# A third set of split weights, a shorter GELU and gate, and new duration formulas in the list scheduler of a two-layer decoder kernel

## The chip, the core and the metric

The kernel runs on one core of a Trainium2 chip. The metric is the device time of one execution in microseconds (us); the median of several runs is given. The engines are named PE (TensorE, the matmuls), PEld (its weight loads), DVE (VectorE), ACT (ScalarE), POOL (GpSimd) and SP (SyncE, whose queue issues the DMAs).

## The reference, cut to what matters

One inference step of a decoder with two layers, 2048 wide, for 592 tokens: 16 meta and 512 prompt tokens (528) and 8 samples of 8 tokens (64). Everything is fp32.

```python
# layer 0: one input projection; a convolution branch and an S5 branch
u_a, g_a, z_a, u_b, z_b = split(x @ ev_w_in)              # 5 x 1024 columns
h   = u_a * sigmoid(g_a)                                  # the gate ("glu")
c   = swish(layernorm(depthwise_conv31(h) + conv_b))      # over 1024 channels
y_a = c @ a_pw
y   = Re(C s5_scan(u_b)) + D * u_b                        # 64 groups of 16, 64 states each
y   = gelu(y)
v, gt = split(y @ glu_w + glu_b);  y_b = v * sigmoid(gt)
mix = concat(y_a * silu(z_a), y_b * silu(z_b))
x   = layernorm(alpha * x + mix @ ev_w_out)
# layer 1: one input projection; mLSTM (4 heads of 256) and RWKV-7 (16 heads of 64)
...
x   = layernorm(alpha * x + mix @ od_w_out)
```

GELU is the tanh form: 0.5 y (1 + tanh(sqrt(2/pi) (y + 0.044715 y^3))). Outputs are the rows of x and the new states of every branch.

## The kernel before

**Dense products.** Features lie on partitions and tokens on columns. Each fp32 product is made of three products of a shorter type (fp32r): the high part of the weights by the high and by the low part of x, and the low part of the weights by the high part of x (in the rows: `acc<-xh,wh`, `acc<-xl,wh`, `acc<-xh,wl`). A weight tile `wraw` (128 x 4 x 128, 256 KB) is loaded by DMA; ACT copies it to `wh`, and DVE subtracts `wh` from it to make `wl`. Each pair feeds 24 matmuls, on 2 column spans of 296 (288 in the RWKV stage). There are two sets of `wh` and `wl`, and a third `wraw` can be loaded ahead. `dense_threads` makes five threads of this: `loads`, `splits`, `products`, `results`, and the jobs that they work through in a fixed order. A job's `then` handles its finished sums in `acc`.

**Order of the work.** Nothing reorders on the chip: each engine runs its queue in program order. The program order within the three manual stages (layer 0; RWKV; mLSTM) comes from a list scheduler, `Weave`. Threads with priorities (a lower number goes first) offer operations; `Weave` keeps a model of every engine's time, takes for each operation the time at which it could start by the model, and emits the one that can start first, priorities deciding among those near each other. The model's durations are in `cost`, and the time from the end of an operation on one engine to the start of its reader on another is in `delay`. So these formulas never change what is computed or how long anything takes; they decide who stands ahead of whom in each queue. Between the stages stand the two output projections, written in a plain order.

**Layer 0.** Jobs: S5 inputs, gates and convolution inputs, gate columns `z`. The S5 branch goes in 8 blocks: tables are made on POOL, PE multiplies (`sps<-s5ul,s5m`, `sps<-s5xpad,s5ca`, `sps<-s5xpad,s5cb`), ACT copies the output to `s5y`, and the GELU of `s5_out` runs over ACT and DVE in tiles `s5q` and `s5y`. `yb` takes the result to DRAM. The convolution's 31 taps are STT (scalar_tensor_tensor) operations on DVE (`taps<-hh,par,taps`). The thread `norms` makes the LayerNorm sums, then waits until all 8 GELU blocks are issued (`len(YB) == 8`), closes the pool that the convolution and S5 used, and makes the operand `C[0]` to `C[7]` of the product `a_pw` one after another: on DVE an STT, on ACT a tanh (`sa`), on DVE a tensor_scalar and an STT (all on `cc`), on ACT the copy `cbh`, on DVE the subtraction `cbl`. The operand Y of the product `glu_w` is loaded back from DRAM and split the same way (`cbh`, `cbl` with strided columns). The first job of `a_pw` needs `C[0]` to `C[7]` in turn (`acc<-cbh`).

**RWKV.** 16 pairs of groups and heads go through: PE products of the group's chunk (`sps<-rar,rbdk` and others); results go through DRAM (`rcd`) and come back as `rcf`; POOL inverts small triangular matrices by a chain of 30 small operations (`rnt<-rcf,rn` and `rn<-rn,rnt`, 15 each); then POOL makes `rlv`, which PE reads. Behind the chain in POOL's queue also stand the low parts `rlo` of the head norms, which PE reads in `sps<-rlo,rcc` and `sps<-rlo,rcb`. A serial chain carries the state over the chunks: `qy<-rgm,rtok`, DVE copies `rqt`, PE transposes (`cp<-cst,rqt`), ACT `rq`, PE `cp<-rtok` and `cp<-rq,rhh`, DVE `rs`, the next `qy`. Dense products of `w_m` and `w_r` fill PE between these. The mLSTM stage follows with the products of `w_g`.

Of the kernel before, what the change touches and what calls it, by code (L numbers as in the profile page):

```python
# [11 lines left out]
F32 = mybir.dt.float32  # L12
# [209 lines left out]
def delay(p, e):  # L222

    if p == e:
        return {"G": 0.1, "D": 2.0}.get(e, 0.0)
    if e == "T":
        return {"A": 0.3, "V": 0.23, "G": 0.2}.get(p, 1.2) + MT
    return {"T": 0.2, "G": 0.08, "D": 1.2}.get(p, 0.14) + (MV if e == "V" else MA)
# [10 lines left out]
def cost(e, fn, out, ins):  # L239

    n = math.prod(out.shape[1:])
    if e == "T":
        if fn == "transpose":
            return 0.12
        return max(n, 256) / 2400 + 0.003 if ins[0].dtype == F32R else max(n / 600 + 0.006, 0.218)
    n = max([n] + [math.prod(z.shape[1:]) for z in ins])
    cols = sum(z.shape[1:] == (1,) for z in ins) * (n > 1)
    if e == "A":
        return 0.05 + n / 1100 + 0.09 * cols
    if e == "G":  # L250
        if fn == "memset":
            return 0.03 + n / 1190
        return 0.13 + n / 300 if fn == "tensor_copy" else max(0.157 + n / 560, 0.055 + n / 417)
    if fn == "reciprocal":
        return 0.07 + n / 160
    fast = fn == "tensor_scalar" and all(z.space != PSUM for z in ins)
    return 0.07 + n / (1920 if fast else 960) + 0.06 * cols

# [333 lines left out]
def s5_setup(K, pool, S):  # L592
# [12 lines left out]
    yield G.memset(S.xpad, 0.0)  # L605
    dt, mag, th = t_("dt"), t_("mag"), t_("th")
    tmp = t_("ean"), t_("ear"), t_("eae", sh, I32)
    yield V.tensor_copy(dt, P["ldt"])
# [3 lines left out]
    yield tt(th, P["lami"], dt, OP.mult)  # L612
    n = t_("n")
    yield V.tensor_scalar(n, th, 1.0 / (2 * math.pi), 12582912.0, op0=OP.mult, op1=OP.add)
# [6 lines left out]
    yield V.tensor_scalar(th, th, 3.1415925, -3.1415925, op0=OP.min, op1=OP.max)  # L621
    sn, cs = t_("sn"), t_("cs")
    yield A.activation(cs, th, AF.Abs)
# [9 lines left out]
    yield V.memset(S.pi[:, :, 0], 0.0)  # L633
    t1, t2 = t_("t1"), t_("t2")
    for k in range(2, 9):
# [167 lines left out]
def s5_out(K, pool, S, j, tables, u, yb, ahead):  # L803
# [30 lines left out]
    q = pool.tile([128, 592], F32, name="s5q", tag="s5u", bufs=4)  # L834
    yield A.square(q, y)
    yield V.tensor_scalar(q, q, 0.044715, 1.0, op0=OP.mult, op1=OP.add)
    yield V.tensor_tensor(q, q, y, op=OP.mult)
    yield A.activation(q, q, AF.Tanh, scale=math.sqrt(2.0 / math.pi))
    yield V.tensor_scalar(y, y, 0.5, None, op0=OP.mult)
    yield V.scalar_tensor_tensor(y, q, 1.0, y, op0=OP.add, op1=OP.mult)  # L840
# [36 lines left out]
def layer0(K, O):  # L877
# [3 lines left out]
    with mk("l0") as p0:  # L881
# [3 lines left out]
        with banks(K, sps=2), mk("ln0") as pl, mk("cc", 8) as pc, mk("zs") as pz, ExitStack() as mid, \  # L885
# [38 lines left out]
            def inputs(j, tag):  # L924
# [10 lines left out]
                return Job(I["w_e"], 24 + j, SPAN0, then, tag=tag, after=after)  # L935

            def glu_gate(j):
                def then(acc):
                    g = cv.tile([128, NT], F32, name="sg")
                    for p, (a, b) in zip(acc, SPAN0):  # L940
                        yield A.activation(g[:, a:b], p, AF.Tanh, scale=0.5)
                    w.give("acc", "acc")
                    yield V.tensor_scalar(g, g, 0.5, 0.5, op0=OP.mult, op1=OP.add)
                    SG.append(g)
                return Job(I["w_e"], 8 + j, SPAN0, then)

            def glu(j):
                b8 = lambda z: z.rearrange("p (b t) -> p b t", b=8)

                def then(acc):  # L950
                    g = SG.popleft()
                    h = cv.tile([128, 862], F32, name="hh", bufs=2)
                    hs = b8(h[:, 558:])
                    yield D.dma_start(hs[:, :, 0:30], I["sconv"][j])
                    yield G.memset(h[:, 0:30], 0.0)
                    yield V.tensor_tensor(h[:, 30:326], g[:, 0:296], acc[0], op=OP.mult)
                    yield V.tensor_tensor(h[:, 326:558], g[:, 296:NP], acc[1][:, 0:232], op=OP.mult)
                    yield V.tensor_tensor(hs[:, :, 30:38], b8(g[:, NP:NT]), b8(acc[1][:, 232:296]), op=OP.mult)
# [5 lines left out]
                return Job(I["w_e"], j, SPAN0, then)  # L964

# [23 lines left out]
            def out(j):  # L989
                def then(acc):  # L990
# [85 lines left out]
            def norms():  # L1076
# [170 lines left out]
class Job:  # L1247
# [3 lines left out]

    def __init__(self, W, s, spans, then, paired=False, final=False, X=None, tag="acc", after=None):
        self.W, self.s, self.spans, self.then, self.paired, self.final = W, s, spans, then, paired, final
        self.after = after
        self.X, self.tag, self.nk = X, tag, W.shape[2] if W is not None else 0


def dense_threads(K, w, jobs, X):


    q = Ctx()
    q.raw, q.w, q.acc, q.nraw, q.nw = deque(), deque(), deque(), 0, 0
    q.loaded, q.freed, q.early = 0, 0, []

# [16 lines left out]
    def splits():  # L1281
        while True:
            yield lambda: q.raw and (q.nw < 2 or q.raw[0] is None)
            item = q.raw.popleft()
# [4 lines left out]
            q.nw += 1  # L1289
            wh, wl = (K.wp.tile([128, 4, 128], F32R, name=m, bufs=2) for m in ("wh", "wl"))  # L1290
            if job.paired:
                yield w.A.copy(wh[:, :, 0:64], raw[:, :, 0:64])
                yield w.V.tensor_tensor(wh[:, :, 64:], raw[:, :, 0:64], wh[:, :, 0:64].bitcast(F32), op=OP.subtract)
            else:
                yield w.A.copy(wh, raw)
                yield w.V.tensor_tensor(wl, raw, wh.bitcast(F32), op=OP.subtract)
            q.nraw -= 1
            q.w.append((wh, wl, job, i0))

    def products():  # L1300
        while True:
            yield lambda: q.w
            item = q.w.popleft()
            if item is None:
                q.acc.append(None)
                return
            wh, wl, job, i0 = item
            if not job.spans:
# [7 lines left out]
            for kk in range(4):  # L1316
# [1051 lines left out]
```

## Time and profile before

| | before |
|---|---|
| median of 3 runs | 2701.41 us (2700.88 to 2701.69) |
| the profiled execution | 2697.97 us; span 2696.0 us |
| mean granted clock of TensorE | 0.986 |
| PE busy | 2586.8 us (96%), 18864 instructions |
| DVE busy | 1637.6 us (61%) |
| ACT busy | 1070.7 us (40%) |
| POOL busy | 1005.3 us (37%) |

The span runs from the first to the last instruction of the profiled execution; its own time is 2 us more. PE is busy nearly all of the time, so the time is the matmuls' work, at the clock that is granted, and PE's idle stretches. Layer 0 runs to about 1030 us (the output projection from about 800), RWKV from there to 1970, mLSTM to about 2480, and the last output projection to the end.

### The profile page before, as it was taken

To read this page: it belongs to the slowest core of one execution; us is meant where nothing else is said; L and a number is where in the kernel's file an instruction comes from. 1 tells how busy PE (TensorE), PEld (TensorE's weight loads), DVE (VectorE), ACT (ScalarE), POOL (GpSimd) and SP (SyncE) were. 2 spreads that over 40 slices of the span, in tenths; PEclk is the share of its full clock that TensorE was granted. 3 is DMA by queue.
4 is the path that set the end of the run, shared out by engine and by line. 5 is a ranking of instruction groups with operands and counts; after the bars stand their busy time and mean duration, and the time that the engine had idled before them with its cause. 6 is when DMAs were issued, how large, how long until landed. Compare 5 with 4: busy or idle time off the path is not lost. (4 is left out here: it accounts for less than half of the span.)

```text
span 2696.0 us, 49549 instructions
## 1 busy us (share of the span) xinstructions
PE 2586.8 (96%) x18864; PEld 2523.7 (94%) x18864; DVE 1637.6 (61%) x3070; ACT 1070.7 (40%) x2313; POOL 1005.3 (37%) x1810
## 2 busy tenths in 40 slices
PE   8998999999999999998999999999999999999997
PEld 8998999899999999998989999999999989898997
DVE  7578986755443356675776757667563544457436
ACT  4322332344232244554554545455333434344223
POOL 1887788720002233343344143244200212212443
PEclk9999999999999999999999999999999999999999
DMA  6433443345333333222222222222333433425333
GB/s 199 104 104 90 110 112 90 103 134 148 110 106 104 107 111 130 80 71 72 71 71 71 75 80 65 69 73 76 97 105 88 140 99 122 145 89 174 109 109 118
DMA packets 202094, 278.31 MB, mean 103 GB/s; under 512 B 66809, under 2 KB 86009, under 8 KB 201857
## 3 DMA queue, kind: packets, MB, share of 16 engines
q1 hardware_dynamic: 199552, 270.30, 33.5%
q10 hardware_dynamic: 2304, 4.85, 0.5%
q8 instruction: 148, 2.42, 0.4%
q14 instruction: 90, 0.73, 0.1%
HBM read 232.54 MB, written 42.53 MB: 102 GB/s over the span
## 5 line engine op out<-in xcount | busy, mean ns | idle before, releaser
L321 PE MATMUL acc<-xh,wh 128*128 128x296 f32 (+1 forms) x3520 | 805.8, 306 | 10.2 <-ACT xh L321 6.5
L321 PE MATMUL acc<-xh,wl 128*128 128x296 f32 (+2 forms) x3488 | 796.4, 305 | 15.2 <-DVE wl L321 15.1
L321 PE MATMUL acc<-xl,wh 128*128 128x296 f32 (+1 forms) x3520 | 802.8, 305 | 0.0
L321 DVE TENSOR_TENSOR wl<-wraw,wh 128x512 fp32r<-128x512 f32 x492 | 385.6, 784 | 373.4 <-ACT wh L321 356.2
L321 PEld LDWEIGHTS acc<-xh,wh 128*128 128x128 f32 x3520 | 584.5, 192 | 15.4 <-ACT xh L321 6.5
L321 PEld LDWEIGHTS acc<-xh,wl 128*128 128x128 f32 x3488 | 577.0, 191 | 19.8 <-DVE wl L321 17.6
L321 PEld LDWEIGHTS acc<-xl,wh 128*128 128x128 f32 x3520 | 583.3, 191 | 1.4 <-issue 0.7
L321 ACT CAST wh<-wraw 128x512 fp32r<-128x512 f32 (+1 forms) x496 | 306.1, 618 | 660.9 <-PE acc L321 592.5
L490 PE MATMUL acc<-xh,wh 128*128 128x296 f32 (+2 forms) x832 | 182.7, 299 | 0.0
L490 PE MATMUL acc<-xl,wh 128*128 128x296 f32 (+2 forms) x832 | 181.9, 297 | 0.7 <-DVE xl L321 0.7
L490 PE MATMUL acc<-xh,wl 128*128 128x296 f32 (+1 forms) x832 | 181.4, 298 | 0.5 <-DVE wl L434 0.5
L321 DVE SCALAR_TENSOR_TENSOR taps<-hh,par,taps 128x528 f32<-128x528 f32 x232 | 178.3, 768 | 4.7
L433 ACT CAST wh<-wraw 128x512 fp32r<-128x512 f32 x100 | 61.9, 621 | 207.8 <-PE acc L490 205.1
L490 PEld LDWEIGHTS acc<-xl,wh 128*128 128x128 f32 x832 | 132.4, 188 | 1.3 <-DVE xl L321 0.9
L490 PEld LDWEIGHTS acc<-xh,wh 128*128 128x128 f32 x832 | 132.4, 189 | 0.5 <-ACT wh L433 0.2
L490 PEld LDWEIGHTS acc<-xh,wl 128*128 128x128 f32 x832 | 131.9, 188 | 0.9 <-DVE wl L434 0.7
L434 DVE TENSOR_TENSOR wl<-wraw,wh 128x512 fp32r<-128x512 f32 x100 | 73.8, 738 | 94.2 <-ACT wh L433 88.6
L321 POOL TENSOR_TENSOR rnt<-rcf,rn 128x75 f32<-128x75 f32 (+14 forms) x240 | 86.5, 360 | 88.7 <-DMA rcf<-rcd 72.3
L404 POOL TENSOR_TENSOR lnb<-lnb,rr 128x592 f32<-128x592 f32 (+1 forms) x24 | 42.4, 1766 | 184.2 <-DVE rr L1155 184.2
L1186 POOL TENSOR_TENSOR rr<-rr,lna 128x592 f32<-128x592 f32 (+1 forms) x2 | 3.5, 1742 | 280.0 <-DMA wraw<-w_eo 254.8
L321 POOL TENSOR_TENSOR k<-mc,mch 128x512 fp32r<-128x512 f32 x32 | 42.9, 1341 | 152.3 <-ACT mch L321 139.8
L321 ACT ACT_TABLE_LOAD x69 | 88.5, 1283 | 18.8 <-DVE rh L321 17.0
(586 smaller groups left out, 4851.9 us busy)
## 6 DMA issues: line engine op xcount, KB each, us to landing
wraw<-w_e SPq DMA_DIRECT2D x160, 256.0 KB, 3.2
wraw<-w_m SPq DMA_DIRECT2D x160, 256.0 KB, 3.1
wraw<-w_r SPq DMA_DIRECT2D x132, 256.0 KB, 3.1
wraw<-w_eo SPq DMA_DIRECT2D x64, 256.0 KB, 3.0
wraw<-w_oo SPq DMA_DIRECT2D x64, 256.0 KB, 3.1
rcf<-rcd SPq DMA_DIRECT2D x16, 640.0 KB
wraw<-w_glu SPq DMA_DIRECT2D x32, 256.0 KB, 2.6
mc<-mc SPq DMA_DIRECT2D x32, 256.0 KB, 3.3
```

The costliest lines, as they stand in the source:

```text
L321: getattr(eng.e, fn)(out, *a, **kw)
L404: getattr(eng.e, fn)(out, *a, **kw)
L433: K.nc.scalar.copy(H, x)
L434: (e or K.nc.vector).tensor_tensor(L, x, H.bitcast(F32), op=OP.subtract)
L490: K.nc.tensor.matmul(o, w[:, kk], x[:, a:b], start=st, stop=sp)
L1186: G.tensor_tensor(r, r, N.c, op=OP.subtract)
```

## The change

Three edits are joined.

1. The formulas in `cost` and `delay` for ACT, POOL and DVE get other numbers. POOL to PE becomes 0.5 instead of 0.2. Small operations become dearer: a DVE operation costs at least 0.2, a POOL operation on two tensors at least 0.25 + n/560, ACT 0.1 + n/1150; an operation of DVE with two tensors in SBUF costs 0.06 more. All three stages are ordered by them.
2. In layer 0 alone there is a third set of split weights (`wh3`, `wl3`, in the pool `cv`): every third split goes there, and up to three split sets may stand ready. Before the pools are closed (`mid.close()`) it must be used up.
3. The GELU of `s5_out` loses two tensor_scalar operations of 128x592 on DVE, and its tensor_tensor becomes an STT; the gate of the convolution loses one tensor_scalar (`sg`). The factors of 0.5 go into the split of the weights `w_glu` and of `w_e`'s first 8 column blocks (`half`): there ACT's copy becomes a multiplication, and DVE's subtraction an STT, in 64 splits. The small temporaries of the S5 set-up are packed in one tile.

```diff
@@ delay
-        return {"A": 0.3, "V": 0.23, "G": 0.2}.get(p, 1.2) + MT
+        return {"A": 0.3, "V": 0.23, "G": 0.5}.get(p, 1.2) + MT
@@ cost
-        return 0.05 + n / 1100 + 0.09 * cols
+        return 0.1 + n / 1150 + 0.06 * cols
...
-        return 0.13 + n / 300 if fn == "tensor_copy" else max(0.157 + n / 560, 0.055 + n / 417)
+        return 0.2 + n / 750 if fn == "tensor_copy" else max(0.25 + n / 560, 0.1 + n / 417)
...
+    if fn == "tensor_tensor_scan":
+        return 0.2 + n / 960
+    if fn == "tensor_reduce":
+        return 0.2 + n / 960
     fast = fn == "tensor_scalar" and all(z.space != PSUM for z in ins)
-    return 0.07 + n / (1920 if fast else 960) + 0.06 * cols
+    both = sum(z.space != PSUM and z.shape[1:] != (1,) for z in ins) > 1
+    return max(0.07 + n / (1920 if fast else 960), 0.2) + 0.06 * cols + 0.06 * both
@@ s5_out
-    yield A.square(q, y)
-    yield V.tensor_scalar(q, q, 0.044715, 1.0, op0=OP.mult, op1=OP.add)
-    yield V.tensor_tensor(q, q, y, op=OP.mult)
+    yield A.activation(q, y, AF.Square, scale=math.sqrt(0.044715))
+    yield V.scalar_tensor_tensor(q, q, 1.0, y, op0=OP.add, op1=OP.mult)
     yield A.activation(q, q, AF.Tanh, scale=math.sqrt(2.0 / math.pi))
-    yield V.tensor_scalar(y, y, 0.5, None, op0=OP.mult)
     yield V.scalar_tensor_tensor(y, q, 1.0, y, op0=OP.add, op1=OP.mult)
@@ norms
                 yield lambda: len(YB) == 8
+                q.closing = True
+                yield lambda: q.own == 0
                 mid.close()
@@ splits
-            yield lambda: q.raw and (q.nw < 2 or q.raw[0] is None)
+            yield lambda: q.raw and (q.nw < 2 + bool(more and not q.closing) or q.raw[0] is None)
...
+            own = more and q.nsplit % 3 == 2 and job.spans and not q.closing
...
+            elif job.half:
+                yield w.A.mul(wh, raw, 0.5)
+                yield w.V.scalar_tensor_tensor(wl, raw, 0.5, wh.bitcast(F32), op0=OP.mult, op1=OP.subtract)
```

The number of instructions stays nearly the same: PE none more or fewer, DVE 24 fewer (8 each of `s5q`, `s5y`, `sg`), ACT 12 more, 4 of them table loads, POOL and SP none.

What the new formulas do to the order is shown at three places; each row is a line of the program, engine operation, out<-in, shape and count. First PE in layer 0, from the last S5 output matmul (`s5xpad,s5cb`) to the first product of `a_pw`. Before:

```order
L321 MATMUL sps<-s5xpad,s5cb 128x148
L321 MATMUL acc<-xh,wl 128x296
L321 MATMUL acc<-xh,wh 128x296 x2
L321 MATMUL acc<-xl,wh 128x296 x2
L321 MATMUL acc<-xh,wl 128x296 x2
```

and so on: 511 dense matmuls stand between that output matmul and the first `acc<-cbh`. In the changed kernel the end of that stretch and the first product of `a_pw` are:

```order
L326 MATMUL acc<-xh,wh 128x296 x2
L326 MATMUL acc<-xl,wh 128x296 x2
L326 MATMUL acc<-xh,wl 128x296 x2
L326 MATMUL acc<-cbh,wh 128x296 x2
L326 MATMUL acc<-cbl,wh 128x296 x2
L326 MATMUL acc<-cbh,wl 128x296 x2
```

36 dense matmuls are left in it: the S5 blocks moved back behind nearly all of the input products.

Second POOL in the RWKV stage, around the end of a chain of `rnt` and `rn` (the third of 16) and the `rlo` of the head norm that PE's `sps<-rlo,rcc` reads. Before:

```order
L321 TENSOR_TENSOR rnt<-rcf,rn 128x5x3
L321 TENSOR_TENSOR rn<-rn,rnt 128x5x3
L321 TENSOR_TENSOR rnt<-rcf,rn 128x5x2
L321 TENSOR_TENSOR rn<-rn,rnt 128x5x2
L321 TENSOR_TENSOR rnt<-rcf,rn 128x5
L321 TENSOR_TENSOR rn<-rn,rnt 128x5
L321 TENSOR_TENSOR rlo<-ry,rhi 128x320
```

Now:

```order
L326 TENSOR_TENSOR rnt<-rcf,rn 128x5x4
L326 TENSOR_TENSOR rlo<-ry,rhi 128x320
L326 TENSOR_TENSOR rn<-rn,rnt 128x5x4
L326 MEMSET rx 128x48
L326 TENSOR_TENSOR rnt<-rcf,rn 128x5x3
L326 TENSOR_TENSOR rn<-rn,rnt 128x5x3
```

This `rlo` stood behind all 30 operations of the chain and stands behind 23. On PE, between the group's last `sps<-rar,rbdk` and the `sps<-rlo,rcc` stand 87 dense matmuls before and 92 now, and up to the first `sps<-rlv` 104 before and 138 now.

Third PE at the end of the RWKV stage, the last step of the serial chain (`cp`, `qy`) and the last head norm (`rhi`, `rlo`). Before, the norm's last two rows among the dense products of `w_r` (columns 288):

```order
L321 MATMUL acc<-xh,wh 128x288 x2
L321 MATMUL sps<-rhi,rcb 128x320
L321 MATMUL acc<-xl,wh 128x288 x2
L321 MATMUL acc<-xh,wl 128x288 x2
L321 MATMUL acc<-xh,wh 128x288 x2
L321 MATMUL sps<-rlo,rcb 128x320
L321 MATMUL acc<-xl,wh 128x288 x2
```

70 dense matmuls of `w_r` stand behind the norm's last row, and up to 20 between each two of its rows. Now:

```order
L326 MATMUL cp<-rtok 128x128
L326 MATMUL cp<-rq,rhh_12494 128x128
L326 MATMUL qy<-rgt__23489,rq 128x64
L326 MATMUL sps<-rhi,rcc 128x320
L326 MATMUL sps<-rlo,rcc 128x320
L326 MATMUL sps<-rhi,rcb 128x320
L326 MATMUL sps<-rlo,rcb 128x320
L326 MATMUL acc<-xh,wh 128x296 x2
L326 MATMUL acc<-xl,wh 128x296 x2
```

The dense products of `w_r` are all used up some steps earlier: the last three steps of the serial chain and the norm stand alone, and the products of `w_g` (columns 296) follow at once.

## Rows read from the trace of the kernel before

**Rows 1.** PE's waits over the whole span: waiting group <- releaser: us, times, longest

```profile
PE sps L321 <- POOL rlo L321: 26.1, 11, 3.4
PE acc L321 <- DVE wl L321: 15.1, 9, 4.2
PE sps L321 <- POOL rlv L321: 7.6, 7, 3.3
PE acc L321 <- ACT xh L321: 6.5, 1, 6.5
```

**Rows 2.** windows: us, then PE, PEld, DVE, ACT, POOL, PEclk, DMA, GB/s

```profile
0.00:600.00 600.00, 569.47 (x4164) 563.79 (x4165) 440.76 (x692) 190.05 (x353) 408.21 (x720) 0.99 0.43 116
600.00:700.00 100.00, 100.00 (x733) 100.00 (x733) 54.10 (x84) 39.22 (x59) 0.00 (x0) 1.00 0.51 141
1050.00:1970.00 920.00, 870.68 (x6497) 844.46 (x6496) 611.79 (x1357) 464.98 (x1132) 340.81 (x843) 0.97 0.25 76
1970.80:1974.20 3.40, 3.40 (x16) 3.40 (x15) 0.00 (x0) 0.09 (x1) 0.00 (x0) 0.50 0.83 196
```

**Rows 3.** one tile's instructions on DVE: `sg`, ns min/median/max

```profile
L321 DVE TENSOR_SCALAR sg<-sg x8: 520/1068/3221, 84.2 to 444.4; 128x592 f32<-128x592 f32 x8
```

**Rows 4.** groups on DVE by form, 100 to 540 us: count, busy us, mean ns

```profile
L321 DVE SCALAR_TENSOR_TENSOR taps<-hh,par,taps 128x528 f32<-128x528 f32 x232 | 178.3, 768 | 4.7
L321 DVE TENSOR_TENSOR wl<-wraw,wh 128x512 fp32r<-128x512 f32 x110 | 105.0, 956 | 64.2 <-ACT wh L321 64.0
```

**Rows 5.** the S5 branch's output matmuls, ns, first and last start

```profile
L321 PE MATMUL sps<-s5xpad,s5cb x64: 288/289/393, 224.7 to 566.3; 128*128 128x148 f32 x64
```

**Rows 6.** matmuls on tile `cbh`, ns, first and last start

```profile
L321 PE MATMUL acc<-cbh,wh x384: 295/300/304, 636.2 to 793.0; 128*128 128x296 f32 x192
```

**Rows 7.** timeline of ACT from 564 us: start, us, instruction

```profile
566.59 0.41 ACT L321 COPY s5y<-sps 128x296 f32<-128x296 f32 x1 [1.77 <-PE sps L321]
```

**Rows 8.** timeline of DVE from 564 us

```profile
572.33 0.83 DVE L321 SCALAR_TENSOR_TENSOR cc<-cc,par,taps 128x592 f32<-128x592 f32 x1
...
575.14 0.77 DVE L321 SCALAR_TENSOR_TENSOR cc<-sa,cc 128x592 f32<-128x592 f32 x1
576.66 0.78 DVE L321 TENSOR_TENSOR cbl<-cc,cbh 128x592 fp32r<-128x592 f32 x1 [0.75 <-ACT cbh L321]
```

**Rows 9.** timeline of DVE from 600 us: a `cbl` of the Y operand

```profile
605.37 1.25 DVE L321 TENSOR_TENSOR cbl<-cc,cbh 128x592 fp32r<-128x592 f32 x1
```

**Rows 10.** timeline of PE from 1184 us

```profile
1190.70 0.39 PE L321 MATMUL sps<-rar,rbdk 128*128 128x128 f32 x2
```

**Rows 11.** timeline of POOL from 1191 us

```profile
1204.09 0.73 POOL L321 TENSOR_TENSOR rnt<-rcf,rn 128x75 f32<-128x75 f32 x1 [2.36 <-DMA rcf<-rcd]
...
1217.20 0.86 POOL L321 TENSOR_TENSOR rlo<-ry,rhi 128x320 fp32r<-128x320 f32 x1
```

**Rows 12.** timeline of PE from 1205 us

```profile
1218.11 0.41 PE L321 MATMUL sps<-rlo,rcc 128*128 128x320 f32 x1 [3.40 <-POOL rlo L321]
```

**Rows 13.** timeline of DVE, end of the RWKV stage

```profile
1947.85 0.45 DVE L321 COPY rqt<-qy 64x64 f32<-64x64 f32 x2
...
1950.89 0.35 DVE L321 SCALAR_TENSOR_TENSOR rs<-cp,rdend,rds 128x128 f32<-128x128 f32 x1 [1.67 <-PE cp L321]
...
1964.00 0.55 DVE L321 SCALAR_TENSOR_TENSOR ry<-ry,k,rbon 128x320 f32<-128x320 f32 x1
```

**Rows 14.** timeline of ACT, end of the RWKV stage

```profile
1949.31 0.28 ACT L321 ACTIVATE rq<-cp 128x128 f32<-128x128 f32 x1 [3.17 <-PE cp L321]
```

**Rows 15.** timeline of PE, end of the RWKV stage

```profile
1947.04 0.38 PE L321 MATMUL qy<-rgm,rtok 128*128 128x128 f32 x2
...
1951.61 0.33 PE L321 MATMUL qy<-rgt__23278,rq 128*128 128x64 f32 x2
...
1957.96 0.31 PE L321 MATMUL sps<-rlo,rcb 128*128 128x320 f32 x1
```

**Rows 16.** timeline of PE where the mLSTM stage begins

```profile
1970.21 0.54 PE L321 MATMUL acc<-xh,wh 128*128 128x296 f32 x2 [2.68 <-DVE wh L321]
```

More of the change, by code (lines that the diff above doesn't have):

```diff
@@ L605, in s5_setup @@
     yield G.memset(S.xpad, 0.0)
-    dt, mag, th = t_("dt"), t_("mag"), t_("th")
-    tmp = t_("ean"), t_("ear"), t_("eae", sh, I32)
+    z = pool.tile([128, 11, 32], F32, name="s5tmp", tag="s5ca", bufs=4)
+    dt, mag, th, ean, ear, eae, n, sn, cs, t1, t2 = (z[:, i] for i in range(11))
+    tmp = ean, ear, eae.bitcast(I32)
     yield V.tensor_copy(dt, P["ldt"])
@@ L612, in s5_setup @@
     yield tt(th, P["lami"], dt, OP.mult)
-    n = t_("n")
     yield V.tensor_scalar(n, th, 1.0 / (2 * math.pi), 12582912.0, op0=OP.mult, op1=OP.add)
@@ L621, in s5_setup @@
     yield V.tensor_scalar(th, th, 3.1415925, -3.1415925, op0=OP.min, op1=OP.max)
-    sn, cs = t_("sn"), t_("cs")
     yield A.activation(cs, th, AF.Abs)
@@ L633, in s5_setup @@
     yield V.memset(S.pi[:, :, 0], 0.0)
-    t1, t2 = t_("t1"), t_("t2")
     for k in range(2, 9):
@@ L935, in inputs, with parts @@
                 return Job(I["w_e"], 24 + j, SPAN0, then, tag=tag, after=after)
+            b8 = lambda z: z.rearrange("p (b t) -> p b t", b=8)
+            def parts(h, acc):
+                return ((h[:, 30:326], acc[0]), (h[:, 326:558], acc[1][:, 0:232]),
+                        (b8(h[:, 558:])[:, :, 30:38], b8(acc[1][:, 232:296])))
             def glu_gate(j):
                 def then(acc):
-                    g = cv.tile([128, NT], F32, name="sg")
-                    for p, (a, b) in zip(acc, SPAN0):
-                        yield A.activation(g[:, a:b], p, AF.Tanh, scale=0.5)
+                    h = cv.tile([128, 862], F32, name="hh", bufs=2)
+                    hs = b8(h[:, 558:])
+                    yield G.memset(h[:, 0:30], 0.0)
+                    yield D.dma_start(hs[:, :, 0:30], I["sconv"][j])
+                    for o, p in parts(h, acc):
+                        yield A.activation(o, p, AF.Tanh, scale=0.5)
                     w.give("acc", "acc")
-                    yield V.tensor_scalar(g, g, 0.5, 0.5, op0=OP.mult, op1=OP.add)
-                    SG.append(g)
+                    SG.append(h)
                 return Job(I["w_e"], 8 + j, SPAN0, then)
             def glu(j):
-                b8 = lambda z: z.rearrange("p (b t) -> p b t", b=8)
                 def then(acc):
-                    g = SG.popleft()
-                    h = cv.tile([128, 862], F32, name="hh", bufs=2)
+                    h = SG.popleft()
                     hs = b8(h[:, 558:])
[L954 to L958, printed above, removed]
+                    for o, p in parts(h, acc):
+                        yield V.scalar_tensor_tensor(o, o, 1.0, p, op0=OP.add, op1=OP.mult)
                     w.give("acc", "acc")
@@ L963, in then @@
                     yield D.dma_start(O["o_conv"][rows, 1:9, :], hs[:, :, 8:38])
-                return Job(I["w_e"], j, SPAN0, then)
+                return Job(I["w_e"], j, SPAN0, then, half=True)
             def gates(s):
@@ L995, in then @@
                     w.give("acc", "acc")
-                return Job(I["w_glu"], j, SPAN0, then, X=Y)
+                return Job(I["w_glu"], j, SPAN0, then, X=Y, half=True)
             def out_gate(j):
@@ L1006, in then @@
                     yield from mixed(z)
-                return Job(I["w_glu"], 8 + j, SPAN0, then, X=Y)
+                return Job(I["w_glu"], 8 + j, SPAN0, then, X=Y, half=True)
             def jobs():
@@ L1126, in loads_y @@
                     Y.append((h, l))
-            q, loads, splits, products, results = dense_threads(K, w, jobs(), X)
+            q, loads, splits, products, results = dense_threads(K, w, jobs(), X, cv)
             w.run([(-1, splits), (-1, splits_x()), (0, results), (1, s5_applied()), (2, s5_tabled()), (3, norms()), (4, loads_y()),
@@ L1247, with __init__, dense_threads @@
 class Job:
-    def __init__(self, W, s, spans, then, paired=False, final=False, X=None, tag="acc", after=None):
+    def __init__(self, W, s, spans, then, paired=False, final=False, X=None, tag="acc", after=None,
+                 half=False):
         self.W, self.s, self.spans, self.then, self.paired, self.final = W, s, spans, then, paired, final
-        self.after = after
+        self.after, self.half = after, half
         self.X, self.tag, self.nk = X, tag, W.shape[2] if W is not None else 0
-def dense_threads(K, w, jobs, X):
+def dense_threads(K, w, jobs, X, more=None):
     q = Ctx()
     q.raw, q.w, q.acc, q.nraw, q.nw = deque(), deque(), deque(), 0, 0
-    q.loaded, q.freed, q.early = 0, 0, []
+    q.loaded, q.freed, q.early, q.nsplit, q.own, q.closing = 0, 0, [], 0, 0, False
     def loads():
@@ L1289, in splits @@
             q.nw += 1
-            wh, wl = (K.wp.tile([128, 4, 128], F32R, name=m, bufs=2) for m in ("wh", "wl"))
+            own = more and q.nsplit % 3 == 2 and job.spans and not q.closing
+            q.nsplit += 1
+            q.own += bool(own)
+            wh, wl = (more.tile([128, 4, 128], F32R, name=m + "3", bufs=1) if own else
+                      K.wp.tile([128, 4, 128], F32R, name=m, bufs=2) for m in ("wh", "wl"))
             if job.paired:
@@ L1297, in splits @@
             q.nraw -= 1
-            q.w.append((wh, wl, job, i0))
+            q.w.append((wh, wl, job, i0, bool(own)))
     def products():
@@ L1306, in products @@
                 return
-            wh, wl, job, i0 = item
+            wh, wl, job, i0, own = item
             if not job.spans:
@@ L1325, in products @@
             q.nw -= 1
+            q.own -= own
             if i0 == job.nk - 4:
```

## The prediction

> **What bounds the kernel now.** I read the busy times first: PE is busy 96% of the span, so a microsecond is won only where PE stands idle or runs at the half clock. Then I read PE's waits, to see who is late, and then windows, to see where. Three things show. In the first 600 us PE is busy 569.5 [rows 2], so it waits 30.5; 15.1 of that is for the low part of the weights, `wl`, and 6.5 is the start, which nothing here touches [rows 1]. From 1050 to 1970 PE waits 49.3 of 920 us [rows 2], and 33.7 of it, 26.1 + 7.6, is for POOL's `rlo` and `rlv` [rows 1]. From 600 to 700 us PE is busy 100%: 733 dense matmuls in 100 us, or 0.136 us each [rows 2]. The granted clock is 0.99 of full in the first stretch and 0.97 in RWKV. Right behind the wait at 1970 us it is 0.50, which is the lower of the two levels, and 16 matmuls begin in 3.4 us where 25 would [rows 2]. A mean of 0.97 made of the levels 1 and 0.5 is 6% of the time at the lower one, 55 us, and half of that lost: some 27 us in RWKV, and 6 in layer 0, at most, since PE also idles in it.
>
> **The shorter GELU and gate, and the third set.** DVE loses 24 operations. One of them, `sg`, takes 0.52 us at best, 1.07 in the median and 3.2 at worst [rows 3]; taken as about 1 us each this frees 25 us of DVE in layer 0, where DVE is busy 441 of 600 us [rows 2]. DVE bounds nothing there on average; what counts is the 15.1 us for `wl`, whose operation takes 0.96 us in the mean while POOL works hard [rows 4]. With a split in reserve, a late `wl` has one more tile's products, 24 matmuls or 3.3 us, to hide behind; the longest of these waits was 4.2 [rows 1]. I leave 2 of the 15.1 (0 to 8), and 3 of the remaining 8.9 of small waits (30.5 - 15.1 - 6.5).
>
> A rule that speaks against this: by the SBUF page of the Trainium skill ("SBUF — State Buffer", section "SBUF: two separate sides") a DVE operation with two SBUF inputs locks GpSimd's port pair or waits for it, whole instructions long. By it the STT forms would be stretched like the subtraction, the 64 new STT splits would be no better off, and the GELU would keep part of its delay. The trace differs in part: 232 STT taps with two SBUF inputs, in the same stretch, take 0.768 in the mean, the subtractions 0.956 at fewer elements [rows 4].
>
> **The changeover in layer 0.** The operand of `a_pw` can be made only after the last GELU. Before, the last S5 output matmul starts at 566.3 [rows 5] and the first `acc<-cbh` at 636.2 [rows 6], 69.9 us later, and the 511 dense matmuls between fill exactly that (511 x 0.136 = 69.5). Now 36 are left, 4.9 us. How long does the operand take without company? From the output matmul to the first STT of `cc` it took 6.0 us before (566.3 to 572.33, by way of `s5y` at 566.59) [rows 5, 7, 8]. Two tensor_scalars of some 0.5 and the weight splits among them go, so I take 4.1. One C goes from 572.33 through 575.14 to the end of `cbl` at 577.44 [rows 8], 5.1 us, 0.6 of it a weight split that now stands in few of the eight. A strided `cbl` of Y (1.25 instead of 0.78) [rows 8, 9] stands in six of the eight. So 4.5 without, 5.0 with: 4.1 + 2 x 4.5 + 6 x 5.0 = 43, and with some splits 45. Under it lie 4.9 of dense work and the 42 products that C[0] to C[6] allow, 5.7 us. PE stands idle for about **34 us**; the bounds are 28 (4.4 each) and 40 (5.6 each). It starts and ends in the half clock as well.
>
> Layer 0: waits 30.5 before; 6.5 + 2 + 3 + 34 = 45.5 now: +15. Of the clock's 6 I keep 4: -2. Together **+13** (+3 to +26).
>
> **RWKV, POOL's chain.** One group as an example: the last `sps<-rar,rbdk` at 1190.70 [rows 10], the chain's first operation at 1204.09, released by the transfer, the `rlo` behind its last at 1217.20 [rows 11], and PE, which has waited 3.40, goes on at 1218.11 [rows 12]. So the results come 27 us after the group's products: 13.4 for the way through DRAM, 13.1 for 30 small operations, 0.9 for `rlo`. The old POOL formula gives these 30 about 10 us, so PE's queue came there too early. The new one gives some 13. In the order, PE's dense work and its small matmuls (at their intervals in the trace) from the group's products to the first `rlv` behind the chain come to 23 to 26 us in nearly all groups before, and to 27.5 to 30.4 in all 16 now. For the `rlo`, which now stand inside the chain where they can, PE's work less what POOL does ahead of them rises by 3.4 in the mean, from 7.2-11.0 to 10.9-14.2, against 13.4 for the way through DRAM, which the formulas leave as short as it was. The mean wait was 2.1 a group (33.7/16). Most are covered; groups at 11 stay 1 to 2 us late. I leave 10 of 33.7 (2 to 18): **-24**. With fewer stops the clock falls less: of 27 I leave 12: **-15** (-5 to -20).
>
> **RWKV, the end.** Before, the serial chain's last `qy<-rgt` starts at 1951.61, the norm's last matmul at 1957.96 [rows 15], `ry` is done at 1964.55 [rows 13], all under products of `w_r`, and PE waits 2.68 for the first split of `w_g` [rows 16]. Now no dense product is left for the last three steps. One step under filler takes from `qy` at 1947.04 [rows 15] over `rqt` at 1947.85 to `rs` at 1950.89 [rows 13] and 0.35 on; PE's own queue holds it up in places, and ACT's part is done at 1949.59 [rows 14]. I take 3.0 bare; 4.2 is the upper bound. The end of the step in hand 1, two steps 6, the third to its `qy<-rgt` 2.6, the norm's matmuls 6, its tail on ACT and DVE 5 (6.6 less two weight splits), `w_g`'s split 0.7: 21.3. PE's own work in it is about 7, so it idles 14.3 instead of 2.7: +11.6, and 1.6 more at the half clock: **+13** (+9 to +18).
>
> **Elsewhere.** mLSTM's last norm has some 25 dense matmuls less in front of the last projection (up to 3.4 us) and small waits that may shrink by 2: **+1**. The projections are written straight and don't change.
>
> **Sum.** +13 - 24 - 15 + 13 + 1 = **-12**. The profiled execution of 2697.97 would become 2686; the median lies 3.4 above it, so 2701.4 becomes **2689**.
>
> **Rivals.**
> *The bubble decides (slower).* The way from the group's products to the chain is 13.4 against slacks of 10.9 to 14.2. If transfers behave as before and PE arrives just as early in real time, POOL's waits stay at 25 and the clock at 22; the gains are 9 + 5, the costs 13 + 13 + 1: +13, 2714. It decides once more than 18 of the 33.7 stay with a clock little better. For it: the transfer's formula is as it was. Against it: every group gained work. Chance 0.17.
> *RWKV comes clean and the changeover is short.* Bubble 28, POOL's waits 2, clock 7: +7 - 32 - 20 + 11 = -34, 2667. For it: the waits are all short (3.4 at most) [rows 1]. Chance 0.18.
> *`wl` stays late.* The third set and the shorter forms move the waits only, because DVE is held up by POOL at each split: 10 of the 15.1 stay, +8 on the forecast: 2697. This is what the page's rule above would give. Chance 0.15.
> The forecast, 2676 to 2696, has 0.50.
>
> **Numbers.** A measurement of this kernel tells about 0.2%, 5.4 us, from no change. The forecast and the clean RWKV are faster (0.47 + 0.18, less 0.03 at its edge); of `wl` late, half is within 0.2%. Slower is the bubble's case, less what ends within 0.2% of it, and the far end of the others. Faster 0.65, same 0.17, slower 0.18. The range reaches from the clean case's middle to just under the bubble's: 2665 to 2713.
>
> **What would show it.** In the changed profile: a stretch of about 45 us near 600 us in which PE is some 25% busy and waits for `cbl`, `cbh` and `cc` in turn; no wait for `wl` above 2 us before it; POOL's `rlo` and `rlv` among PE's waits with 10 us instead of 33.7; a granted clock of 0.98 to 0.99 from 1050 us to the end of RWKV; about 14 us of waits in the last 21 before `w_g`. I am wrong if PE's dense work goes on through the changeover, if the waits on POOL are above 20, or if DVE's new forms are stretched as the subtraction was.

## The result, and the profile after

The changed kernel takes 2662.85 us (median of 4 runs, 2660.69 to 2665.85) against 2701.14 (4 runs, 2697.31 to 2701.69): 0.9853 of the time, 95% interval 0.9838 to 0.9867, 38 us less. The prediction was 2689, with a range from 2665 to 2713: the direction was right, and the time lies 2 us under the range.

The page's first lines for the changed kernel (engine, busy us, share of the span, instructions):

```profile
span 2658.9 us, 49536 instructions
PE 2574.2 (97%) x18864; PEld 2513.6 (95%) x18864; DVE 1636.3 (62%) x3046; ACT 1077.8 (41%) x2325; POOL 1002.3 (38%) x1810
```

PE's waits over the whole span, the answer to [rows 1]:

```profile
PE acc L326 <- ACT cbh L326: 17.7, 7, 3.4
PE acc L326 <- ACT xh L326: 6.2, 1, 6.2
PE acc L326 <- DVE wh L326: 4.8, 1, 4.8
PE sps L326 <- POOL rlo L326: 4.7, 5, 1.7
PE sps L326 <- ACT rh L326: 4.2, 5, 1.4
...
PE sps L326 <- POOL rlv L326: 0.4, 1, 0.4
```

The wait for `wl` has left the list (15.1 before), `rlo` and `rlv` fall from 33.7 to 5.1, and the head of the list is new: `cbh`, the operand of `a_pw` at the changeover from layer 0's input products to `a_pw`. Windows of the changed kernel, with the columns of [rows 2]: the changeover alone and with what lies around it, all from there to the last chunks of RWKV, RWKV's end, and mLSTM's first products:

```profile
600.00:700.00 100.00, 77.02 (x478) 71.74 (x477) 57.01 (x85) 38.65 (x54) 7.11 (x5) 0.80 0.45 115
...
605.00:655.00 50.00, 27.02 (x118) 21.74 (x118) 34.78 (x51) 25.18 (x34) 2.11 (x2) 0.61 0.47 105
657.00:1915.00 1258.00, 1244.58 (x9405) 1222.53 (x9403) 793.12 (x1643) 587.85 (x1334) 410.18 (x893) 1.00 0.30 92
1911.00:1938.00 27.00, 15.50 (x75) 10.48 (x73) 17.12 (x39) 9.04 (x23) 5.27 (x13) 0.73 0.08 27
1938.20:1944.20 6.00, 6.00 (x25) 6.00 (x26) 0.61 (x2) 0.41 (x1) 0.00 (x0) 0.51 0.57 141
```

From 657 to 1915 us PE idles 13, and the clock is never granted at the lower level. From the changeover to mLSTM's first products nearly all that is lost stands in two places, at 605 to 655 and at 1911 to 1944, and there the granted clock is 0.51 to 0.73.

To compare kernels I cut each profiled execution at the same matmuls: layer 0 ends with the last product of `cbh`, RWKV runs from the first `qy` to the first product of `w_g`, mLSTM from there to its last norm. The projection between layer 0 and the first `qy` takes 234.7 us in both, the rest after mLSTM's norm 217.5 and 217.9.

| us | before | after | difference | predicted |
|---|---|---|---|---|
| layer 0 | 793.9 | 806.0 | +12.1 | +13 |
| RWKV | 941.7 | 897.5 | -44.2 | -26 |
| mLSTM | 508.3 | 502.9 | -5.4 | +1 |

So layer 0 was foreseen, and the gains in RWKV and mLSTM were under-valued. Executions of different kernels that share a stage's order differ in that stage's time by up to 3.6 us (in the table of runs below, layer 0 under the old formulas with three sets: 784.9 to 788.2; RWKV under all the new formulas: 897.4 to 901.0, without e10 and e11), so smaller differences between stage times tell nothing.

**The changeover.** The last S5 output matmul and the products of the new operand (ns; first and last start):

```profile
L326 PE MATMUL sps<-s5xpad,s5cb x64: 287/289/454, 281.3 to 607.7; 128*128 128x148 f32 x64
L326 PE MATMUL acc<-cbh,wl x384: 294/299/502, 617.2 to 805.7; 128*128 128x296 f32 x192
```

and PE there (timeline: start, us, instruction, idle before it and its releaser):

```profile
616.16 0.71 PE L326 MATMUL acc<-cbh,wh 128*128 128x296 f32 x2 [3.24 <-ACT wh L326]
...
621.30 0.86 PE L326 MATMUL acc<-cbh,wh 128*128 128x296 f32 x2 [3.39 <-ACT cbh L326]
...
625.83 0.86 PE L326 MATMUL acc<-cbh,wh 128*128 128x296 f32 x2 [2.36 <-ACT cbh L326]
...
630.61 0.86 PE L326 MATMUL acc<-cbh,wh 128*128 128x296 f32 x2 [2.36 <-ACT cbh L326]
```

PE gets one block C of the operand every 4.5 to 5.1 us, as worked out (4.5 and 5.0), and the first STT of `cc` starts at 611.60, 3.9 us behind the output matmul (4.1 worked out). PE stands idle for 23 of the 50 us, not 34: at the lower clock the products between the waits last twice as long and fill the rest. Since the operand sets the pace, this adds nothing to the loss; the two together cost what the idle time alone was to cost: in 100 us, from 600 to 700, PE issues 478 matmuls, where it issued 733 [rows 2], and 255 at 0.136 are 34.7 us. The same row for the time at the lower level alone:

```profile
616.40:657.30 40.90, 21.15 (x66) 16.12 (x66) 31.02 (x42) 20.12 (x25) 0.00 (x0) 0.50 0.50 106
```

**RWKV's end**, as [rows 15, 16] showed it before:

```profile
1927.23 0.53 PE L326 MATMUL qy<-rgt__23489,rq 128*128 128x64 f32 x2
1928.60 0.63 PE L326 MATMUL sps<-rhi,rcc 128*128 128x320 f32 x1 [0.85 <-ACT rhi L326]
...
1932.68 0.64 PE L326 MATMUL sps<-rlo,rcb 128*128 128x320 f32 x1 [0.30 <-POOL rlo L326]
1938.11 0.86 PE L326 MATMUL acc<-xh,wh 128*128 128x296 f32 x2 [4.79 <-DVE wh L326]
```

From the last dense product at 1912.3 to the first of `w_g` it takes 25.8 us; 21.3 were predicted.

### The profile page after: what moved, and what is told of

It is laid out like the page before. It is cut to its first block, busy times and chain, and to the rows that moved or that the text cites. A ratio compares the mean times of both kernels' runs of the same rounds, so it can differ in the third digit from the quotient of the medians.

```text
span 2658.9 us, 49536 instructions
## 1 busy us (share of the span) xinstructions
PE 2574.2 (97%) x18864; PEld 2513.6 (95%) x18864; DVE 1636.3 (62%) x3046; ACT 1077.8 (41%) x2325; POOL 1002.3 (38%) x1810
## 4 chain that ended last, share of the span: by engine, by line
PE 87%; DVE 4%; DMA 3%; POOL 2%; ACT 2%; issue 2%; SPq 1%; ACTq 0%; DVEq 0%; POOLq 0%
PE acc L326 53%; PE sps L326 13%; PE acc L495 12%; PE acc L468 3%; DMA rcf<-rcd 2%; PE cp L326 1%; PE qy L326 1%; SPq L326 1%; PE pb L326 1%; DVE wl L326 1%; POOL rnt L326 1%; POOL rn L326 1%; DVE taps L326 0%; PE sps L409 0%; DVE rr L1207 0%
## 5 line engine op out<-in xcount | busy, mean ns | idle before, releaser
L326 PE MATMUL acc<-xh,wh 128*128 128x296 f32 (+1 forms) x3520 | 798.9, 303 | 11.6 <-ACT xh L326 6.2
L326 DVE TENSOR_TENSOR wl<-wraw,wh 128x512 fp32r<-128x512 f32 x428 | 338.1, 791 | 291.3 <-ACT wh L326 272.5
L326 ACT CAST wh<-wraw 128x512 fp32r<-128x512 f32 x432 | 266.8, 618 | 583.9 <-PE acc L326 492.2
L438 ACT CAST wh<-wraw 128x512 fp32r<-128x512 f32 x100 | 61.7, 620 | 203.7 <-PE acc L495 201.0
L439 DVE TENSOR_TENSOR wl<-wraw,wh 128x512 fp32r<-128x512 f32 x100 | 72.7, 730 | 92.0 <-ACT wh L438 86.4
L326 PE MATMUL acc<-cbh,wh 128*128 128x296 f32 x384 | 87.6, 311 | 20.9 <-ACT cbh L326 17.7
```

The lines of the kernel that those rows point to most:

```text
L326: getattr(eng.e, fn)(out, *a, **kw)
L438: K.nc.scalar.copy(H, x)
L439: (e or K.nc.vector).tensor_tensor(L, x, H.bitcast(F32), op=OP.subtract)
```

## The experiments

All of them start from one of the two kernels and choose by stage which of the new formulas are used: G (POOL) and T (POOL to PE), V (DVE), A (ACT). Each was timed in 3 rounds beside the kernel before; the stage times are from its profiled execution.

```diff
+NEW = set("GVAT")      # emptied and filled anew ahead of each stage
...
-        return 0.1 + n / 1150 + 0.06 * cols
+        return 0.1 + n / 1150 + 0.06 * cols if "A" in NEW else 0.05 + n / 1100 + 0.09 * cols
```

| run | layer 0 by | RWKV by | mLSTM by | us | ratio (95%) | layer 0 | RWKV | mLSTM |
|---|---|---|---|---|---|---|---|---|
| e1, without the other edits | all new | all new | all new | 2683.6 | 0.9944 (0.9926-0.9961) | 824.8 | 897.4 | 502.5 |
| e2 | old | old | old | 2692.3 | 0.9983 (0.9971-0.9994) | 787.4 | 943.3 | 507.6 |
| e3 | old | all new | all new | 2642.0 | 0.9788 (0.9774-0.9803) | 786.0 | 899.5 | 502.2 |
| e4 | old | G, T | old | 2656.1 | 0.9838 (0.9818-0.9858) | 787.0 | 903.7 | 510.0 |
| e5 | old | V, A | old | 2695.0 | 0.9980 (0.9970-0.9989) | 786.2 | 947.3 | 507.2 |
| e6 | old | G, T, V | all new | 2649.4 | 0.9810 (0.9792-0.9828) | 788.0 | 905.7 | 501.5 |
| e7, two sets | all new | all new | all new | 2666.6 | 0.9877 (0.9862-0.9891) | 805.9 | 897.9 | 502.9 |
| e8 | G, T, A | all new | all new | 2645.8 | 0.9800 (0.9782-0.9817) | 790.6 | 897.5 | 503.3 |
| e9, two sets | old | all new | all new | 2654.0 | 0.9824 (0.9805-0.9843) | 792.1 | 901.0 | 502.7 |
| e10, POOL +4 | old | all new | all new | 2672.1 | 0.9894 (0.9876-0.9913) | 788.2 | 927.9 | 501.6 |
| e11, POOL +8 | old | all new | all new | 2700.4 | 0.9996 (0.9982-1.001) | 784.9 | 948.3 | 504.2 |
| e12, chain's end on DVE | old | G, T | all new | 2671.2 | 0.9891 (0.9868-0.9915) | 785.4 | 928.8 | 500.0 |

**Which part does it: e1 and e2.** In e1 the kernel before gets the formulas alone, in e2 the changed kernel keeps the old ones.

> The kernel before with nothing but the new duration formulas, in all three stages. Theory A (the formulas bring the gain, in the RWKV stage, and cost something in layer 0): RWKV about 44 us shorter from its first to its last matmul, mLSTM 5 shorter, and in layer 0 an idle stretch at the changeover of 35 to 40 us that no longer wait for split weights offsets; 2672 us (2660 to 2688). Theory B (the third set and the shorter GELU and gate bring it): no faster than 2692.

> The changed kernel with the old formulas in all stages, so that only the third set and the shorter GELU and gate are left. Theory A: RWKV and mLSTM as before, no idle stretch at the changeover (546 dense matmuls stand there), only layer 0's waits for split weights go: 2686 us (2678 to 2694). Theory B: 2670 or less.

The formulas take RWKV from 942 to 897 and mLSTM from 508 to 502.5; the other edits do nothing there (943.3, 507.6). Theory B falls. Both expected times were some 6 to 12 us too low. In e1 layer 0 grows by 31 us. The waits of its first 640 us begin with these two, and the second is this matmul's:

```profile
PE acc L331 <- DVE wl L331: 16.1, 6, 4.2
PE acc L331 <- ACT wh L331: 10.2, 1, 10.2
```

```profile
636.90 0.86 PE L331 MATMUL acc<-cbh,wh 128*128 128x296 f32 x2 [10.17 <-ACT wh L331]
```

So the wait for `wl` stays as it was before (15.1), and the 10.2, put down to `wh`, stand in front of the first product of `a_pw`: they belong to the changeover, where e1's order leaves no dense matmul. The expectation of e7 below adds the two up to 26 us of waits for split weights; 16 of them are that.

**Old order in layer 0, new behind it: e3 and e8.**

> The changed kernel with the old formulas in layer 0 and the new ones in RWKV and mLSTM. Theory A: both gains and not the idle stretch: about 25 us under the changed kernel, 2637 us (2628 to 2646). Theory B (the idle stretch is the third set's doing, which puts the splits ahead of the S5 blocks): the stretch stays and the time is 2655 or more.

> The changed kernel with DVE's old formulas in layer 0 and all else new. 201 dense matmuls stand at the changeover, 27 us of cover against 4.9 with 36 and 74 with 546. Theory F1 (the idle stretch is the operand's 45 us less the cover): some 22 us of it go, and layer 0 takes 786 to 792 us; 2642 us (2636 to 2650). Theory F2 (the loss in layer 0 comes from elsewhere, waits for weights among others): layer 0 800 us or more, 2655 or more.

Theory A and F1 hold: the stretch at the changeover comes from the formulas in layer 0, DVE's above all, and shrinks with the dense matmuls left for it: 36, 201 and 546 of them go with 806.0, 790.6 and 786.0 us of layer 0 in kernels that differ in nothing else there (e1, with none, has 824.8, but also the long GELU and the waits for `wl`). With 201 PE is busy 38.4 of the 50 us from 600 (window of e8):

```profile
600.00:650.00 50.00, 38.37 (x240) 35.89 (x239) 37.32 (x54) 26.12 (x37) 0.00 (x0) 0.83 0.53 126
```

The 165 matmuls of cover, 22 us, brought 15.4. e3 is the fastest of all: 2642.0 us, 21 under the changed kernel.

**Which formula does it in RWKV: e4, e5 and e6.**

> Third set and shorter GELU and gate, old formulas everywhere but in the RWKV stage, where the POOL formulas and the POOL to PE delay alone are new. Theory A1 (POOL's chain of 30 small operations was modelled too short, and that is the whole of RWKV's gain): waits on POOL under 10 us there, no lower clock, and dense products left for the stage's end, so no idle stretch of 14 us there either: 2633 us (2624 to 2646). Theory A2 (the DVE and ACT formulas space the serial chain and bring half or more of it): 2660 or more, waits on POOL above 15 us.

> As the run with the POOL formulas alone, but in RWKV the DVE and ACT formulas are new and those of POOL old. With the POOL formulas alone RWKV took 903.7 us, with all 897 to 899, with none 942. Theory C1 (POOL's waits are the gain; DVE and ACT add to it only once these are gone): PE still waits 20 us or more for POOL, RWKV 925 us or more, and its end has an idle stretch; 2678 us (2668 to 2692). Theory C2 (either set of formulas spaces the chain enough): RWKV 910 us or less, 2660 us or less.

> The changed kernel with the old formulas in layer 0, and in RWKV those of POOL and DVE new and that of ACT old; mLSTM all new. In its order all steps of the serial chain at RWKV's end keep dense products beside them, and only the last four matmuls of the norm stand bare. Theory D1 (the idle stretch at RWKV's end costs about 13 us and comes from the dense products running out): RWKV 886 us (880 to 894), 2631 us (2622 to 2640). Theory D2 (what is not lost at the end is lost in waits earlier): RWKV 897 or more, 2640 or more.

The same 850 us of RWKV in before, e5, e4 and the changed kernel (windows, one row each in this order):

```profile
1050.00:1900.00 850.00, 806.52 (x6018) 782.38 (x6018) 576.53 (x1283) 439.35 (x1075) 322.40 (x791) 0.97 0.24 74
```

```profile
1050.00:1900.00 850.00, 806.28 (x6046) 785.03 (x6045) 576.97 (x1281) 439.82 (x1067) 320.13 (x790) 0.97 0.25 75
```

```profile
1050.00:1900.00 850.00, 824.66 (x6274) 798.44 (x6274) 605.24 (x1339) 461.07 (x1116) 347.59 (x842) 0.99 0.26 78
```

```profile
1050.00:1900.00 850.00, 836.65 (x6424) 816.46 (x6423) 599.43 (x1314) 455.58 (x1101) 336.08 (x828) 1.00 0.27 82
```

The numbers behind x are PE's instructions: 6018 before, 6424 after. DVE's and ACT's formulas alone bring nothing (e5: PE waits 32.6 us for `rlo` and `rlv`, RWKV 947). POOL's alone, with the delay from POOL to PE, bring 38 to 40 of the 44 us (e4); the durations and the delay were not tried apart. C1 holds for RWKV, though e5's time came out 3 us above its range; A1 holds for the cause, and its time was 10 us above the range. In e6 the filled end of RWKV (D1) was not worth its 13 us: RWKV takes 905.7, more waits stand ahead (6.6 us for ACT's `rh`, 9.5 for POOL), and D2 holds. The dense products are one store, and what covers the end can be missing earlier; but e6 also keeps ACT's old formula, and how much of its waits is due to that was not tried.

**The third set and the shorter GELU: e7 and e9.**

```diff
-            q, loads, splits, products, results = dense_threads(K, w, jobs(), X, cv)
+            q, loads, splits, products, results = dense_threads(K, w, jobs(), X)
```

> The changed kernel with two sets of split weights instead of three; shorter GELU and gate, and all the new formulas, stay. PE's order is the same at the changeover (36 dense matmuls). Layer 0 took 806.0 us with all, 824.8 with the formulas alone, of which waits for split weights are 26. Theory E1 (the third set takes those waits away): layer 0 about 822 us, 2679 us (2672 to 2686). Theory E2 (the 24 DVE operations fewer do): layer 0 about 808, 2665 us (2659 to 2671).

> The run with the old formulas in layer 0 and the new ones behind it (2642.0 us; layer 0 786.0), with two sets of split weights instead of three. If the third set is worth nothing in layer 0 in either order, as 805.9 against 806.0 with the new formulas says: 2642 us (2638 to 2647), layer 0 within 2 us of 786. If it is the third set that brought layer 0 from 793.9 to 787 under the old formulas: layer 0 791 or more, 2648 or more.

In e7 PE's whole order is that of the changed kernel. With the new formulas the third set is worth nothing in layer 0 (805.9 against 806.0), as E2 says, though the wait for `wl` is 6.6 us without it and gone with it: in its place PE waits for transfers (of `w_e` 2.4, of S5's operands 1.6 and 1.6). The third edit (GELU, gate and halved weights) takes layer 0 from 824.8 (e1) to 805.9 (e7) there: DVE is busy 525.3 us in it instead of 549.2, the wait for `wl` falls from 16.1 to 6.6, and the first wait of the changeover from 10.2 to 3.2. With fewer operations to place, the scheduler also leaves 36 dense matmuls at the changeover instead of none; what of the 19 us is that, and what is DVE's missing work, these runs don't separate. With the old formulas the second expectation holds: two sets 792.1, three 786.0, before 793.9. There too the wait for `wl` is gone with three sets, but PE waits for POOL instead, in e3:

```profile
PE sps L331 <- POOL s5xpad L331: 8.3, 2, 4.5
```

Half of e9's 12 us over e3 is layer 0; the other half is spread over RWKV (1.5), mLSTM and the last projection (3.3) and the difference of runs, and stays open.

**How much room the new order has: e10 and e11.** 4 (8) of the operations of each chain run twice, with nothing else moved (PE's order is e3's, matmul by matmul):

```diff
         yield tt(G, t, cf[:, 0:n, :, n].rearrange("p s c -> p c s"), bc(N[:, :, n:n + 1], [128, 5, n]), OP.mult)
+        if n >= 12:        # e11: n >= 8
+            G.e.tensor_tensor(t, cf[:, 0:n, :, n].rearrange("p s c -> p c s"), bc(N[:, :, n:n + 1], [128, 5, n]), op=OP.mult)
```

> Old formulas in layer 0, new ones behind it, and in each of the 16 POOL chains 4 operations run twice, which the scheduler does not count: some 1.6 us more per chain with every other order unchanged. Theory G1 (the new order leaves POOL's results only just in time, and each us of lateness is paid as wait and again in part as lower clock): PE's waits on POOL rise from 6 to about 16, 2656 us (2649 to 2664). Theory G2 (the new order has room of several us per group): 2642 us (2638 to 2647).

> The same with 8 operations run twice, some 3.1 us more per chain, as much as the new formula had added. Theory G1: waits on POOL 25 to 35 us, the lower clock back in 8 or more stretches of RWKV, 2680 us (2668 to 2692). Theory G2: 2650 us or less, no lower clock before RWKV's end.

The chain's mean, from the first operation's start to the last one's end, is 13.5 us in e3, 15.4 in e10 and 17.1 in e11. RWKV grows by 28.4 and 48.8 us, that is 0.92 and 0.86 of the 16 x 1.9 = 31 and 16 x 3.55 = 57 added. G1 holds, and was still too mild: both times came out above its ranges. In e11 PE idles 36 us more than in e3 up to RWKV's last dense product, and the lower clock stands in seven stretches ahead of that instead of two, worth some 8 us more. The waits that answer in e11:

```profile
PE sps L331 <- POOL rlo L331: 21.4, 14, 3.2
PE sps L331 <- POOL rlv L331: 9.5, 7, 3.2
```

So the new order has next to no room there: 3.5 us per chain, about what the new formula had added to the model, take the whole gain back.

**A shorter chain: e12.** For n up to 7 the two operations go to DVE:

```diff
-        yield tt(G, t, cf[:, 0:n, :, n]...
+        yield tt(V if n <= 7 else G, t, cf[:, 0:n, :, n]...
```

> Old formulas in layer 0, those of POOL alone in RWKV, all new in mLSTM (with the old ones in mLSTM this took 2656.1 us, RWKV 903.7, of which mLSTM's formulas are worth 6 to 8), and in each of the 16 chains the last 14 of the 30 small operations on DVE instead of POOL. On POOL these 14 take about 5 us. Theory H1 (RWKV is paced by the way from PE's products over POOL back to PE, nearly one for one): the way gets 1 to 2 us shorter per group, and of 30 us that POOL's way could give back RWKV takes some 15, down to its own work: RWKV 885 to 893, 2636 us (2628 to 2643), faster than all others. Theory H2 (DVE's queue, 70% busy, holds the small operations up behind its splits, as long as POOL took): RWKV 900 to 910, 2646 to 2656 us.

Neither: RWKV takes 928.8. A DVE operation is short here (0.19 and 0.17 us in the median), but DVE's queue stands still while the chain's head is not done; of DVE's waits and of PE's in RWKV:

```profile
DVE rnt L331 <- POOL rn L331: 23.8, 12, 4.1
```

```profile
PE cp L331 <- DVE rqt L331: 10.3, 13, 1.8
PE acc L331 <- DVE wh L331: 6.0, 1, 6.0
PE acc L331 <- DVE wl L331: 6.0, 3, 3.3
```

PE's waits for POOL nearly go (1.1 us), and others, behind the waiting DVE, take their place: `rqt` was 3.2 in e4. The 6.0 for `wh` stand at the stage's end, where e4 has 2.4.

## Why the prediction was right or wrong

**The third set, GELU and gate.** "I leave 2 of the 15.1": 0 are left in the changed kernel. The reason was half right: under the new formulas the third edit alone takes the wait from 16.1 to 6.6 (e7), and the third set only turns the rest into waits for transfers. The 25 us of DVE's time that were to be freed are there between e1 and e7 (23.9), but not between the two kernels: DVE is busy 533.9 us in layer 0 before and 532.5 now, as the new formulas' order lengthens operations on it (549.2 in e1, which has them alone). And one of the prediction's signs of being wrong came true: the new STT forms are stretched as the subtraction was. I had set them apart from it by the taps. The rows of the changed kernel, its first 600 us on DVE (count, busy us, mean ns), contradict that:

```profile
L326 DVE SCALAR_TENSOR_TENSOR taps<-hh,par,taps 128x528 f32<-128x528 f32 x232 | 178.4, 769 | 5.4
L326 DVE TENSOR_TENSOR wl<-wraw,wh 128x512 fp32r<-128x512 f32 x128 | 119.8, 939 | 109.3 <-ACT wh L326 105.7 <-PE acc L326 2.7
L326 DVE SCALAR_TENSOR_TENSOR wl<-wraw,wh 128x512 fp32r<-128x512 f32 x32 | 33.9, 1060 | 15.9 <-ACT wh L326 15.8
L326 DVE SCALAR_TENSOR_TENSOR s5y<-s5q,s5y 128x592 f32<-128x592 f32 x7 | 15.5, 2217 | 1.5 <-ACT s5q L326 0.8 <-DMA s5ul<-ub 0.8
```

The taps stay at 0.77, but the STT split takes 1.06 in the mean. Sorted by what POOL does meanwhile, it takes 1.40 in the mean (median 0.92) while POOL is busy for over nine tenths of it, the subtraction 1.20 (0.94), and both take 0.69 with POOL idle. The last STT of the GELU takes 2.2; it is no new form (1.07 at most before), and seems to wait in place of the removed tensor_scalar ahead of it, which took up to 2.5 before. The taps are spared on both sides: under them POOL's `s5c<-s5a,s5xv` takes 0.36 us, with DVE idle 0.35, and where a `wl` covers three tenths of it or more 0.59. Here the page "SBUF — State Buffer" of the Trainium skill (section "SBUF: two separate sides"), by which a DVE operation with two SBUF inputs and a GpSimd operation that reads SBUF shut each other out, was the better guide for the new forms, and the taps are the exception that it doesn't explain.

**The changeover.** Right in place, mechanism and price: 34 us predicted, 34.7 lost. Only the division was other: PE idles 23 us of it, and slow matmuls fill the rest of a stretch whose length the operand sets. Layer 0 +12.1 for +13. e3 and e8 show that the cover decides it.

**RWKV, POOL's chain: the step that failed.** The mechanism was right (e4, e5, e10, e11), the terms of the sum were too small. RWKV up to its last dense product, before and now (window rows, with the columns of [rows 2]):

```profile
1028.50:1967.20 938.70, 891.85 (x6654) 865.85 (x6653) 621.96 (x1379) 470.24 (x1141) 346.16 (x851) 0.97 0.25 77
```

```profile
1040.70:1912.30 871.60, 858.25 (x6594) 837.86 (x6594) 614.86 (x1348) 466.53 (x1126) 342.78 (x840) 1.00 0.28 83
```

PE's idle time falls from 46.9 to 13.3 us, by 34 where the prediction has 24. The clock gives back 22 us where it has 15: before, the trace shows the lower level for 47.8 us in ten stretches, with PE busy in 43.7 of them (half of that is lost), and now it shows none. Three terms were mis-sized. "Of 27 I leave 12": nothing is left there, and the 27, named as the most, were 22. "I leave 10 of 33.7": 5.1 are left for `rlo` and `rlv`; `rlo` is still late five times, two of them at the stage's end, by 1.7 us at most. And I put at nothing two other waits of PE in the old RWKV, of 8.9 us, of which none is left ahead of the stage's end:

```profile
PE cp L321 <- DVE rqt L321: 5.9, 4, 2.8
PE qy L321 <- DVE rs L321: 3.0, 2, 1.6
```

Whether these two came of POOL's late results wasn't tried apart (e4 leaves 3.2 for `rqt`). RWKV takes 18 us less than forecast and mLSTM 6 less; these are nearly the whole miss of 25 us (-37 between the two profiled executions, -12 forecast).

**RWKV's end.** +13 predicted; 25.8 us instead of 3.0 from the last dense product to `w_g`:

```profile
1912.30:1938.10 25.80, 14.20 (x62) 9.22 (x61) 15.92 (x37) 8.69 (x22) 4.80 (x11) 0.72 0.08 29
```

PE idles 11.6 us of it instead of 2.7 (14.3 predicted), and is busy 14.2, some 11 by the full clock, where the prediction has 7. By the 11 the end costs +12, by the 7 +16. Right in place and nearly in size; filling most of it, as e6 does, didn't win it back.

**mLSTM.** +1 predicted, -5.4 measured. Its own formulas do it (500 to 504 with them, 507 to 510 without), and the wait for `mqz` falls from 3.6 to 0.3; which of the formulas it is wasn't tried. So the sign was wrong here. The shorter cover in front of the last projection, which I priced at up to 3.4, can't be seen in the time (217.5 and 217.9 us behind the norm).

**The rivals.** The clean RWKV with a short changeover came nearest (2667): RWKV was clean, and the changeover was not short. The bubble did not decide. `wl` late was wrong on the wait; its cause, splits on DVE stretched while POOL works, is in the rows above.

## What to carry to other kernels

A list scheduler's duration for a slow engine need not be exact, but where it is too short, the bound engine's queue arrives too early, and each microsecond by which its results come late is paid nearly in full, once per group (here 0.86 to 0.92 of it, e10 and e11). First correct the formula of the engine that the bound engine waits for; the others brought nothing here before it (e5). Such formulas act on every stage: look at each stage's order apart, and keep the new ones where they help (2642 us here, against 2663 with them everywhere). Dense work that fills gaps is a store; where an order has used it up ahead of a serial stretch, the stretch stands bare, here at a granted clock of 0.72.

## What the runs showed of the hardware

At the changeover the lower clock was granted for 41 us, and PE was busy for 21 of them; since the operand set the pace, no loss of its own can be seen in it (34.7 us lost, 34 foreseen from the pace alone). In the old RWKV it cost some 22 us. It doesn't follow PE's idle time in proportion: up to RWKV's last dense product PE idles 46.9 us before and 49.0 in e11, and the lower level is granted for 47.8 us and for 23.9. The row of e11:

```profile
1019.70:1943.00 923.30, 874.35 (x6594) 849.16 (x6593) 611.55 (x1348) 466.87 (x1126) 384.80 (x968) 0.99 0.26 78
```

What kept it up there is open. STT operations on DVE are stretched while POOL works in two places (the split and the GELU, means 1.06 and 2.2 us) and not in a third (the taps, 0.77, with POOL not held up either); why the taps are spared wasn't tried.
